# The second feed-forward as seven block products a tile, its residual kept in DRAM

## The chip, the cores and the metric

The kernel runs on one core of a Trainium2 chip and computes one decoder layer. The metric is the device time of one execution in microseconds (us); the time before is the median of three runs. Engines are named as the profile names them: PE is TensorE (matrix products, with its weight loads as PEld), DVE is VectorE, ACT is ScalarE, POOL is GpSimd, SP is SyncE, which starts most DMAs. SBUF and PSUM are the core's two on-chip memories; PE writes into PSUM, in 8 banks of 512 fp32 columns.

## The reference, cut to what matters

```python
def swiglu(u, w_in, w_out):
    ...                          # silu(u @ gate half of w_in) * (u @ up half of w_in), then @ w_out

def decoder_layer(x, c, lp, attend, s0_re, s0_im):
    ...
    h = x + 0.5 * g1[:, None, :] * swiglu(rms_modulate(x, lp['norm_ffn1'], sh1, sc1),
                                          lp['ffn1_w_in'], lp['ffn1_w_out'])
    ...                          # token mixer: attention and a state space model
    h = h + 0.5 * g3[:, None, :] * swiglu(rms_modulate(h, lp['norm_ffn2'], sh3, sc3),
                                          lp['ffn2_w_in'], lp['ffn2_w_out'])
```

The model width is 1024, the feed-forward's inner width 2816. There are 1024 prompt tokens and 64 tokens of samples, held together as T = 1092 columns (four are zeros). Everything is fp32 in DRAM.

## The kernel before, in words

Activations lie feature by partition: x is [128, 8, 1092], 8 tiles of 128 features (KD = 8). fp32 precision is had from fp16 products: each operand is scaled by a power of two and split into a high and a low fp16 part, and a product is three passes, high·high, high·low and low·high (`passes`, L155). `split` (L92) makes the parts: ACT writes the high one (L94), DVE the low one (L95).

The second feed-forward (`ffn`, L376, called at the end of the kernel) has 22 tiles of the inner width. `up(i)` (L382) makes one: a gate product and an up product, each over 8 k-tiles, 3 passes and 3 chunks of the columns (364, 364 and 360 wide) into one PSUM tile of three banks (`unit`, L165, matmul at L171, two such tiles). ACT takes the silu of the gate (L387), DVE multiplies it with the up product (L390) and takes the absolute maximum of the tile h (L395, `hm`). The first two tiles go chunk by chunk (`up_two`, L400), after the norm's chunks.

The inner width is worked off in three parts, PARTS (L26): tiles 0 to 10, 11 to 17, 18 to 21. When a part's tiles are there, `halves` (L424) takes the part's maximum over the partitions on POOL (L81), and splits each h into fp16 parts in a new slot of the pool hp3 (tag h, 17 slots, L1439). `down(0)` (L436) multiplies the first part with its rows of w_out, one tile of x after the other, and `add_gated` (L354) adds the result to x in SBUF. One more tile, tile 11, goes ahead of `down(0)` to cover the splitting, and `halves(1)`, `halves(2)`, `down(1)` and `last_part` (L461) stand at the end. The first feed-forward is the same code with 15 slots (L1320).

Weights come in groups of up to 1 MB (`Weights`, L99): fetched by SP two groups ahead into two slots wf, measured by DVE (L88), POOL (L81) and three short DVE instructions (L73 to L75), and split one group ahead into two slots each of wh and wl. So `next()` for tile i issues the split of tile i + 1.

Each engine runs its own queue in order. The order in the queues is settled when the program is built, by a scheduler that goes by modelled times and by which slots are free; the code only gives the dependencies. `after_mix` (L1417) makes the operand u of the second feed-forward from x, chunk by chunk, at the end of the mixer (`modulate_chunk`, L309).

Of the kernel before, what the change touches and what calls it, by code (L numbers as in the profile page):

```python
# [20 lines left out]
P = 128  # L21
# [4 lines left out]
PARTS = ((0, 11), (11, 18), (18, 22))  # L26
# [6 lines left out]
T = 3 * CH  # L33
EPS = 1e-6
# [34 lines left out]
def pow2_scale(k, m, pool=None, tag="sc", bufs=8):  # L69
# [21 lines left out]

def split(k, hi, lo, src, s):  # L92
    """hi + lo = s * src to 22 bits."""
    r = k.nc.scalar.activation(hi, src, AF.Copy, scale=s)  # L94
    k.nc.vector.scalar_tensor_tensor(lo, src, s, hi, op0=ALU.mult, op1=ALU.subtract)  # L95
    return r.ins


class Weights:  # L99
    """The groups of weights in the order in which they are used: split one ahead, loaded and measured two ahead.  # L100
    The last group of a product, of twice the size, is kept in slots of the scope's own, aside from the ring."""
# [5 lines left out]
    def fetch(self):  # L107
        k = self.k
        src, nk, nm, *aside = self.order.pop(0)
        wf = []  # L110
        for part in [src[:, :nk // 2], src[:, nk // 2:]] if aside else [src]:
# [3 lines left out]
        self.fetched.append((wf, nm, bool(aside)))  # L115

    def measure(self):
# [3 lines left out]
        for i, f in enumerate(wf):  # L121
# [38 lines left out]
def width(c, first):  # L160
    """Columns of chunk c that a pass takes: the zeros after the last token only need the first one."""
# [3 lines left out]
def unit(k, w, cols, act, nk):  # L165
    """One output tile: [P, 3, CH] of PSUM = sum over nk k-tiles of w[:, :, cols]^T act."""
# [9 lines left out]
def product(k, ps, w, cols, act, nk, c):  # L176
    """ps [P, CH] = chunk c of the columns of such a tile."""
# [37 lines left out]
def ada_part(k, dr, part, queue=None, then=None):  # L215
    """mods[:, part * 8 + tile, sequence]: one part of the modulation."""
# [25 lines left out]
def norm_coef(k, i, gain):  # L242
    """Modulation i as u * s = n * A + B, with s a power of two: A, B and 1 / s."""
# [9 lines left out]
    s, inv = pow2_scale(k, allmax(k, bound), k.co, f"ns{i}", 1)  # L253
# [9 lines left out]
def square_sums(k, x, c):  # L263
    """The sums of squares of the columns of chunk c of x [P, KD, T]: PSUM [4 x 32 equal rows, CH / 4]."""
# [12 lines left out]
def rstd_chunk(k, x, c, ss=None):  # L277
    """1 / rms of these columns, on all partitions: PSUM [P, CH]."""
# [6 lines left out]
    # the inverse square root: half the exponent's bits, then Newton's steps  # L285
# [16 lines left out]
def normalize_chunk(k, x, c, bc=None):  # L302
    """x[:, :, chunk c] to unit root mean square, in place."""
# [43 lines left out]

def scaled_gate(k, gate, iv):
# [5 lines left out]
def add_gated(k, xm, ps, g):  # L354
    """xm [P, T] += g * ps, g [P, NSQ] by sequence, ps [P, 3, CH]."""
# [12 lines left out]
def ffn_order(wi, wo):  # L368
    o = [(wi[i], KD, 256) for i in range(NFF)]
    a, b, c = wo  # L370
    oa = [(a[m], 11, P) for m in range(KD)]
    ob = [(b[g], 7, 256) for g in range(KD // 2)]
    return o[:12] + oa + o[12:] + ob + [(c, 4, D, True)]


def ffn(k, x, u, ivu, gate, fill, after_chunk, between=None):  # L376
    """x += gate * SwiGLU(u); after_chunk(c) is called when the columns of chunk c are complete."""
# [22 lines left out]
    def up_two():  # L400
        """The first two tiles, chunk by chunk of the columns."""
# [59 lines left out]
def last_part(k, x, gate, act, inv, behind, after_chunk):  # L461
    """x += gate * product of the last four k-tiles, chunk by chunk of the columns."""
# [46 lines left out]
def vec_exp(k, pool, x):  # L509
    """exp of a small tile [P, NG] by range reduction and a polynomial."""  # L510
# [16 lines left out]
def ssm_params(k, dr, sp, co):  # L527
    """The transition's powers and the discretized input matrix."""
# [1004 lines left out]
```

## Time and profile before

| | |
|---|---|
| median of 3 runs | 2501.14 us (2498.15 to 2502.89) |
| span of the profiled execution | 2513.7 us, 12.6 above that median |
| PE busy | 2430.5 us, 97% of the span |
| DVE, ACT, POOL busy | 56%, 31%, 7% |
| second feed-forward | the last 750 us or so of the span |

The page states no other time for the profiled execution than its span. How to read it: the span runs from the first instruction to the last on the slowest core; busy shares are of that span. The clock in a profile's window is the TensorE clock that was granted, as a share of full speed. "Idle before" in a row is the time the engine waited just before those instructions, with what ended the wait.

### The profile page before, as it was taken

Reading aid. Unit: us, or ns where it says so; the run is one execution under the profiler, and the core shown is the slowest. Engines: PE = TensorE matmul, PEld = TensorE weight load, DVE = VectorE, ACT = ScalarE, POOL = GpSimd, SP = SyncE. Lnnn points to the kernel's source line nnn. Section 1 sums busy time; section 2 is a strip of 40 time slices with the busy share of each in tenths; the row PEclk is TensorE's granted clock in tenths of the full one; section 3 lists DMA queues with packets and bytes.
Section 4 is the critical chain, followed back from the end, with each engine's and each line's share of the span. In section 5 each row is a group of like instructions: output and inputs, shape, how many; then the busy total and the mean of one; then the engine's idle time right before and its main releaser. Section 6 shows DMA issues by size and latency. Waiting matters only on the chain.

```text
span 2513.7 us, 38505 instructions
## 1 busy us (share of the span) xinstructions
PE 2430.5 (97%) x16615; PEld 1456.6 (58%) x16615; DVE 1417.2 (56%) x2637; ACT 782.4 (31%) x905; POOL 168.2 (7%) x249
## 2 busy tenths in 40 slices
PE   6999999999999999999999899999999999999997
PEld 2555566666656565775444444655666656666564
DVE  4522355458676744638889787697333353333545
ACT  3311122111122432146778676324211221111303
POOL 0111000000000000001133200000000000000000
PEclk8999999999999999889999999999999999999999
DMA  9644101112112234444133214520111111111112
GB/s 349 220 184 168 51 24 55 62 62 88 59 57 99 89 98 147 104 149 157 66 110 104 96 41 148 210 68 18 34 51 51 36 47 62 51 48 35 45 35 72
DMA packets 81946, 229.41 MB, mean 91 GB/s; under 512 B 11680, under 2 KB 45856, under 8 KB 72560
## 3 DMA queue, kind: packets, MB, share of 16 engines
q1 hardware_dynamic: 67952, 179.96, 21.0%
q0 software_dynamic: 13376, 46.70, 5.3%
q8 instruction: 130, 2.13, 0.3%
q10 hardware_dynamic: 448, 0.29, 0.1%
q14 instruction: 40, 0.33, 0.0%
HBM read 190.68 MB, written 36.24 MB: 90 GB/s over the span
## 4 chain that ended last, share of the span: by engine, by line
PE 42%; DVE 6%; ACT 4%; issue 2%; DMA 1%; another core or an unknown queue 1%; POOL 0%; DVEq 0%; POOLq 0%; ACTq 0%
PE u L171 27%; PE u L181 8%; PE z L850 2%; PE o L868 1%; PE P L787 1%; DVE mx L88 1%; PE P L863 1%; DVE h L95 1%; DVE wl L95 1%; DMA wf<-in_w_in 0%; ACT tmp L325 0%; DMA wf<-in_w_out_b 0%; ACT ae L857 0%; PE z L911 0%
## 5 line engine op out<-in xcount | busy, mean ns | idle before, releaser
L171 PEld LDWEIGHTS <-wh 128*128 128x128 f16 x6144 | 589.3, 97 | 387.3 <-issue 38.5
L171 PE MATMUL u<-u,wh 128*128 128x364 f16 (+1 forms) x4032 | 740.6, 317 | 0.0
L171 PE MATMUL u<-u,wl 128*128 128x364 f16 (+1 forms) x2016 | 420.1, 315 | 0.0
L181 PE MATMUL u<-u,wh 128*128 128x364 f16 (+1 forms) x1632 | 393.5, 319 | 12.0 <-ACT u L327 6.3
L171 PEld LDWEIGHTS <-wl 128*128 128x128 f16 x3072 | 298.9, 98 | 176.1 <-issue 2.6
L94 ACT ACTIVATE wh<-wf,sc 128x2048 f16<-128x2048 f32 (+3 forms) x92 | 172.1, 1871 | 681.8 <-PE u L171 616.5
L88 DVE TENSOR_REDUCE mx<-wf 128x1 f32<-128x2048 f32 (+3 forms) x98 | 208.7, 2131 | 250.3 <-DMA wf<-in_ffn_w_in 156.6
L171 PE MATMUL u<-h,wh 128*128 128x364 f16 (+1 forms) x1728 | 315.7, 317 | 9.9 <-DVE h L95 6.1
L181 PE MATMUL u<-u,wl 128*128 128x364 f16 (+1 forms) x816 | 260.2, 319 | 1.1 <-DVE wl L95 1.1
L181 PEld LDWEIGHTS <-wh 128*128 128x128 f16 x1824 | 176.5, 98 | 126.0 <-issue 28.6
L390 DVE SCALAR_TENSOR_TENSOR h<-u,iv,sil 128x1092 f32<-128x1092 f32 x40 | 54.2, 1354 | 331.6 <-PE u L171 293.8
L95 DVE SCALAR_TENSOR_TENSOR wl<-wf,sc,wh 128x2048 f16<-128x2048 f32 (+3 forms) x92 | 200.7, 2182 | 47.3 <-ACT wh L94 46.8
L81 POOL PARTITION_ALL_REDUCE am<-mx x106 | 49.4, 472 | 1966.7 <-DVE mx L88 1880.2
L171 PE MATMUL u<-h,wl 128*128 128x364 f16 (+1 forms) x864 | 180.1, 316 | 0.0
L387 ACT ACTIVATE sil<-u,iv 128x1092 f32<-128x1092 f32 x40 | 46.9, 1171 | 385.3 <-PE u L171 385.3
L181 PEld LDWEIGHTS <-wl 128*128 128x128 f16 x912 | 89.4, 98 | 69.8 <-issue 18.5
L181 PEld LDWEIGHTS <-aside 128*128 128x128 f16 x864 | 83.0, 97 | 50.4 <-issue 1.2
L181 PE MATMUL u<-h,aside 128*128 128x364 f16 (+1 forms) x576 | 90.9, 317 | 0.0
L358 DVE SCALAR_TENSOR_TENSOR x<-u,gt,x 128x728 f32<-128x728 f32 x40 | 38.8, 971 | 87.7 <-PE u L171 87.7
L227 PE MATMUL s<-aw,cs 128*32 128x256 f32 x576 | 64.8, 406 | 11.2 <-DMA aw<-in_ada_w 11.1
L857 ACT ACTIVATE ae<-z,bias,csqk 128x512 f32<-128x512 f32 (+3 forms) x96 | 62.9, 666 | 40.7 <-PE z L855 18.8
L858 DVE TENSOR_SCALAR az<-z,csqk,bias 128x512 f32<-128x512 f32 (+3 forms) x96 | 64.4, 674 | 8.8 <-ACT ae L857 8.2
(375 smaller groups left out, 2583.5 us busy)
## 6 DMA issues: line engine op xcount, KB each, us to landing
wf<-in_ffn_w_in SPq DMA_DIRECT2D x44, 1024.0 KB, 4.9
aw<-in_ada_w POOLq DMA_DIRECT2D x56, 512.0 KB, 6.6
wf<-in_w_in SPq DMA_DIRECT2D x16, 1024.0 KB, 5.6
wf<-in_ffn_w_out_a SPq DMA_DIRECT2D x16, 704.0 KB, 4.1
x<-in_xT SPq DMA_DIRECT2D x6, 1456.0 KB, 14.1
sg<-gd SPq DMA_DIRECT2D x16, 546.0 KB, 5.5
aw<-in_ada_w SPq DMA_DIRECT2D x16, 512.0 KB, 8.3
gd<-gate SPq DMA_DIRECT2D x45, 182.0 KB, 1.9
```

The source lines that it names most:

```text
L81: k.nc.gpsimd.partition_all_reduce(r, m, P, ABSMAX)
L88: k.nc.vector.tensor_reduce(m, src, axis=axis, op=ALU.max, apply_absolute_value=True)
L94: r = k.nc.scalar.activation(hi, src, AF.Copy, scale=s)
L95: k.nc.vector.scalar_tensor_tensor(lo, src, s, hi, op0=ALU.mult, op1=ALU.subtract)
L171: k.nc.tensor.matmul(ps[:, c, :n], wt[:, cols], act(kt, part)[:, c * CH:c * CH + n], start=kt == 0 and j == 0, stop=kt == nk - 1 and j == 2)
L181: k.nc.tensor.matmul(ps[:, :n], wt[:, cols], act(kt, part)[:, c * CH:c * CH + n], start=kt == 0 and j == 0, stop=kt == nk - 1 and j == 2)
L227: nc.tensor.matmul(ps[32 * i:32 * i + 32, :], k.cs[:, 4 * kk + j, :], ws[i][:, j, :], start=kk + j == 0, stop=kk == 1 and j == 3)
L387: nc.scalar.activation(c3(sil), pg, AF.Silu, scale=iv)
L390: nc.vector.scalar_tensor_tensor(c3(h), pu, iv, c3(sil), op0=ALU.mult, op1=ALU.mult)
L850: nc.tensor.matmul(ps[:, :n], a[r, P * j:P * j + P], b[r, cols], start=i == 0, stop=True, skip_group_check=True)
L857: nc.scalar.activation(ae[:, h, :n], ps[:, :n], AF.Abs, scale=inv, bias=b)
L858: nc.vector.tensor_scalar(az[:, h, :n], ps[:, :n], inv, b, op0=ALU.mult, op1=ALU.add)
```

## The change

It touches the second feed-forward, and PARTS for both.

- PARTS becomes 10, 8 and 4 tiles, so tile 10 is the one ahead of `down(0)`.
- Tiles 0 to 3 of the second feed-forward stay plain products, now in PSUM tiles of two banks (`pair_tile`, three of them), and for tiles 2 and 3 by halves of the columns (546, as matmuls of 272 and 274 columns to either side of the bank's border).
- Tiles 4 to 21 are seen as a 2 x 2 block product: rows gate and up, inner blocks of 4 k-tiles, columns in two halves. Seven block products of 4 k-tiles x 3 passes take the place of eight (`seven_products`), accumulated in three PSUM tiles X, Y and Z, with five additions on DVE, one copy and two silus on ACT and a last multiply on DVE.
- These need sums of weights, four DVE instructions of 512 columns a tile and 1536 more columns to split (`Weights.seven`; the layout reorders the weights into blocks), and sums of x, made once during tiles 2 and 3 (`Factors.sums`): 16 DVE sums of 546 columns and 8 splits of 1092, kept in 8 slots of the pool.
- `modulate_chunk` now works in place in x. So x goes to DRAM first (xd, three DMAs), `down(0)` reads each row tile from there and writes it back, and x is loaded again after the last of the seven products of tile 21. x's SBUF becomes a second pool of 8 slots, hq4 (`after_sums`).
- The maximum of |h| is replaced by a sum of |h| on ACT (`abs_bound`), and some scales are four times smaller (`lead=12`).

The diff, without the hunks that only remove comments and without repeated plumbing:

```diff
-PARTS = ((0, 11), (11, 18), (18, 22))
+PARTS = ((0, 10), (10, 18), (18, 22))
...
+def abs_bound(k, src, out):
+    junk = k.tmp().rearrange("p a n -> p (a n)").bitcast(BF16)[:, :src.shape[1]]
+    k.nc.scalar.activation(junk, src, AF.Abs, accum_out=out)
...
+        seven = aside == "seven"
+        fs = [wf[0][:, :1024], wf[0][:, 1024:]] if seven else wf
+        for i, f in enumerate(fs):
             absmax(k, f, mx[:, i:i + 1])
-        m = absmax(k, mx) if aside else mx[:, :1]
-        self.loaded.append((wf, nm, aside, *pow2_scale(k, allmax(k, m))))
+        m = absmax(k, mx) if len(fs) > 1 else mx[:, :1]
+        self.loaded.append((wf, nm, aside, *pow2_scale(k, allmax(k, m), lead=12 if seven else 14)))
...
+        if aside == "seven":
+            self.ready.append((self.seven(wf[0], s), inv, False))
+            return
...
+    def seven(self, f, s):
+        k = self.k
+        v = k.nc.vector
+        a11, a12, a22, a21 = (f[:, i:i + 512] for i in range(0, 2048, 512))
+        t, t4 = (k.tmp().rearrange("p a n -> p (a n)") for _ in range(2))
+        s3, s2, s4 = t[:, :512], t[:, 512:1024], t4[:, :512]
+        v.tensor_sub(s3, a11, a21)
+        v.tensor_add(a21, a21, a22)
+        v.tensor_sub(s2, a21, a11)
+        v.tensor_sub(s4, a12, s2)
+        h, l = (k.wp.tile([P, 2048], F16, tag=t_, bufs=2) for t_ in ("wh", "wl"))
+        split(k, h, l, f, s)
+        h3, l3 = (k.w3.tile([P, 1536], F16, tag=t_, bufs=2) for t_ in ("w3h", "w3l"))
+        split(k, h3[:, :1024], l3[:, :1024], t[:, :1024], s)
+        split(k, h3[:, 1024:], l3[:, 1024:], s4, s)
+        cut = lambda a, i: a[:, 512 * i:512 * i + 512]
+        r = {n: (cut(h, i), cut(l, i)) for i, n in enumerate(("a11", "a12", "a22", "s1"))}
+        r.update({n: (cut(h3, i), cut(l3, i)) for i, n in enumerate(("s3", "s2", "s4"))})
+        return r
...
+def pair_tile(k):
+    return k.psu.tile([P, 1024], F32, tag="u", bufs=3)
+def halves_unit(k, w, cols, act, nk):
+    for h in range(2):
+        ps = pair_tile(k)
+        a0 = h * HT - 240
+        for kt in range(nk):
+            for j, (wt, part) in enumerate(passes(w, kt)):
+                for a, b in ((240, 512), (512, 786)):
+                    k.nc.tensor.matmul(ps[:, a:b], wt[:, cols], act(kt, part)[:, a0 + a:a0 + b],
+                                       start=kt == 0 and j == 0, stop=kt == nk - 1 and j == 2)
+        yield h, slice(h * HT, h * HT + HT), ps[:, 240:786]
...
+        t = src if keep else k.tmp()[:, :nk, :n]
...
+    def sums(self, k, x, g):
+        nc = k.nc
+        v = nc.vector
+        a, b = (k.sum_slot() for _ in range(2))
+        q = x.rearrange("p (q k) (h n) -> p k q h n", q=2, h=2)[:, g]
+        v.tensor_sub(a[:, 0], q[:, 0, 1], q[:, 0, 0])
+        v.tensor_sub(a[:, 1], q[:, 1, 1], q[:, 0, 1])
+        v.tensor_sub(b[:, 0], q[:, 1, 1], a[:, 0])
+        v.tensor_sub(b[:, 1], q[:, 1, 0], b[:, 0])
+        for src in (a, b):
+            t = k.factor_slot()
+            nc.scalar.activation(t[:, :, 0], src, AF.Copy)
+            v.tensor_sub(t[:, :, 1], src, t[:, :, 0])
+            self.t.append(t)
...
+def seven_products(k, w, fac, iv, h):
+    nc = k.nc
+    v = nc.vector
+    view = lambda t: t[:, 240:786]
+    def add(t, a, b, first):
+        ah, al = w[a]
+        act = fac.get(b)
+        for kt in range(4):
+            for j, (wt, part) in enumerate(((ah, 0), (ah, 1), (al, 0))):
+                for c0, c1 in ((240, 512), (512, 786)):
+                    nc.tensor.matmul(t[:, c0:c1], wt[:, kt * P:kt * P + P], act(kt, part)[:, c0 - 240:c1 - 240],
+                                     start=first and kt == 0 and j == 0, stop=kt == 3 and j == 2,
+                                     skip_group_check=True)
+    q = k.sum_slot()
+    u2 = k.u2.tile([P, HT], F32, tag="u2", bufs=2)
+    p1, u3 = q[:, 0], q[:, 1]
+    h1, h2 = h[:, :HT], h[:, HT:]
+    X = pair_tile(k)
+    add(X, "a11", "b11", True)
+    nc.scalar.activation(p1, view(X), AF.Copy)
+    Y = pair_tile(k)
+    add(Y, "s2", "t2", True)
+    v.tensor_add(u2, view(Y), p1)
+    add(X, "a12", "b21", False)
+    nc.scalar.activation(h1, view(X), AF.Silu, scale=iv)
+    add(Y, "s3", "t3", False)
+    v.tensor_add(u3, view(Y), p1)
+    Z = pair_tile(k)
+    add(Z, "s1", "t1", True)
+    v.tensor_add(u3, view(Z), u3)
+    add(Y, "a22", "t4", False)
+    v.tensor_add(p1, view(Y), p1)
+    add(Z, "s4", "b22", False)
+    v.tensor_add(h2, view(Z), u2)
+    nc.scalar.activation(h2, h2, AF.Silu, scale=iv)
+    hh = h.rearrange("p (a n) -> p a n", a=2)
+    v.scalar_tensor_tensor(hh, q, iv, hh, op0=ALU.mult, op1=ALU.mult)
...
+def ffn_seven(k, fac, ivu, gate, xu, xd, after_sums, after_chunk):
+    nc = k.nc
+    hs, hm = {}, {}
+    act = lambda kt, part: fac.u[:, kt, part, :]
+    def bound(i):
+        p = [a <= i < b for a, b in PARTS].index(True)
+        if p not in hm:
+            hm[p] = k.small.tile([P, 12], F32, tag="hm", bufs=3)
+        j = i - PARTS[p][0]
+        abs_bound(k, hs[i], hm[p][:, j:j + 1])
+    def up(i):
+        w = k.w.next()
+        iv = mul_small(k, w[1], ivu)
+        h = hs[i] = k.h_slot(i, [P, T], F32, "h")
+        if i >= PLAIN:
+            seven_products(k, w[0], fac, iv, h)
+        else:
+            for _, cols, ps in halves_unit(k, w, slice(0, P), act, KD):
+                nc.scalar.activation(h[:, cols], ps, AF.Silu, scale=iv)
+            for _, cols, ps in halves_unit(k, w, slice(P, 2 * P), act, KD):
+                nc.vector.scalar_tensor_tensor(h[:, cols], ps, iv, h[:, cols], op0=ALU.mult, op1=ALU.mult)
+        bound(i)
...
+    def halves(p):
+        a, b = PARTS[p]
+        s, inv = pow2_scale(k, allmax(k, absmax(k, hm[p][:, :b - a])), tag="sh", bufs=3)
+        parts = []
+        for i in range(a, b):
+            h2 = k.h_slot(i, [P, 2, T], F16, "h2")
+            ins = split(k, h2[:, 0, :], h2[:, 1, :], hs[i], s)
+            if i - a < 6:
+                behind = ins
+            parts.append(h2)
+        return lambda kt, part: parts[kt][:, part, :], inv, behind
+    def down(p, hact, inv, behind, rows):
+        nk = PARTS[p][1] - PARTS[p][0]
+        per = 1 + p
+        last = [behind, behind]
+        for m in range(KD):
+            if m % per == 0:
...
+                iv = mul_small(k, w[1], inv)
+            xm, done = rows(m, last[m])
+            g = scaled_gate(k, gate[:, m, :], iv)
+            for h, _, ps in halves_unit(k, w, slice(m % per * P, m % per * P + P), hact, nk):
+                ins = add_gated_half(k, xm, h, ps, g)
+            last.append(ins)
+            done()
+    def row(m, after):
+        t = k.hp.tile([P, T], F32, tag="h", name="xr")
+        with k.tc.issue_after(after):
+            nc.sync.dma_start(t, xd[:, m, :])
+        return t, lambda: nc.sync.dma_start(xd[:, m, :], t)
+    up_two()
+    for i in range(2, PLAIN):
+        up(i)
+        n = 4 // (PLAIN - 2)
+        for g in range(n * (i - 2), n * (i - 1)):
+            fac.sums(k, xu, g)
+    after_sums()
+    for i in range(PLAIN, PARTS[0][1] + 1):
+        up(i)
+    down(0, *halves(0), row)
+    for i in range(PARTS[0][1] + 1, NFF):
+        up(i)
+    x = k.up.tile([P, KD, T], F32, tag="u", name="x")
+    for m in range(KD):
+        nc.sync.dma_start(x[:, m, :], xd[:, m, :])
+    h1, h2 = halves(1), halves(2)
+    down(1, *h1, lambda m, _: (x[:, m, :], lambda: None))
+    last_part(k, x, gate, *h2, lambda c: after_chunk(c, x))
...
-            modulate_chunk(k, x, box["cf"], box["u"], c, rstd_chunk(k, x, c))
-        with again(name="ring3", bufs=4) as k.ring:
+            nc.sync.dma_start(xd[:, :, c * CH:(c + 1) * CH], x[:, :, c * CH:(c + 1) * CH])
+            modulate_chunk(k, x, box["cf"], box["u"], c, rstd_chunk(k, x, c), keep=True)
...
+            k.h_slot = lambda i, shape, dt, name: (k.hp if i < 4 or 12 <= i < 17 else k.hq).tile(shape, dt, tag="h",
+                                                                                                 name=name)
+            xs2 = ExitStack()
+            def after_sums():
+                xs.close()
+                k.hq = xs2.enter_context(again(name="hq4", bufs=8, side="right"))
```

## Rows read from the trace of the kernel before

**Rows 1.** Page, part 1: busy us, share of the span, instructions, by engine.
```profile
PE 2430.5 (97%) x16615; PEld 1456.6 (58%) x16615; DVE 1417.2 (56%) x2637; ACT 782.4 (31%) x905; POOL 168.2 (7%) x249
```

**Rows 2.** Stretch table: length; PE, PEld, DVE, ACT, POOL busy (count); clock, DMA.
```profile
1800.00:2514.00 714.00, 693.46 (x4625) 433.76 (x4623) 295.52 (x427) 128.85 (x107) 13.47 (x34) 0.99 0.14 48
```

**Rows 3.** Timeline of PE within one tile: start, us, what, count.
```profile
2166.06 1.09 PE L171 MATMUL u<-u,wh 128*128 128x364 f16 x6
2166.99 0.62 PE L171 MATMUL u<-u,wl 128*128 128x364 f16 x3
...
2171.61 1.09 PE L171 MATMUL u<-u,wh 128*128 128x364 f16 x6
```

**Rows 4.** PE in the mixer, 256 columns: timeline, and its weight loads grouped.
```profile
1088.02 0.38 PE L1107 MATMUL z<-wh,u 128*128 128x256 f16 x2
...
1091.95 0.38 PE L1107 MATMUL z<-wh,u 128*128 128x256 f16 x2
L1107 PEld LDWEIGHTS <-u 128*128 128x128 f16 x384 | 37.9, 99 | 5.5 <-issue 0.4
```

**Rows 5.** DVE groups by form: count, busy us, mean ns of one, idle before.
```profile
L88 DVE TENSOR_REDUCE mx<-wf 128x1 f32<-128x2048 f32 x72 | 164.3, 2283 | 186.0 <-DMA wf<-in_ffn_w_in 156.6 <-DMA wf<-in_ffn_w_out_c 18.2 <-DMA wf<-in_w_in 9.5
L95 DVE SCALAR_TENSOR_TENSOR wl<-wf,sc,wh 128x2048 f16<-128x2048 f32 x66 | 154.8, 2345 | 41.0 <-ACT wh L94 40.4
L390 DVE SCALAR_TENSOR_TENSOR h<-u,iv,sil 128x1092 f32<-128x1092 f32 x40 | 54.2, 1354 | 331.6 <-PE u L171 293.8 <-PE s L618 26.3 <-issue 11.5
L358 DVE SCALAR_TENSOR_TENSOR x<-u,gt,x 128x728 f32<-128x728 f32 x40 | 38.8, 971 | 87.7 <-PE u L171 87.7
L784 DVE SCALAR_TENSOR_TENSOR ae<-ae,csqk,ah 128x1024 f16<-128x1024 f32 x24 | 33.7, 1405 | 2.7 <-issue 1.6 <-DVE az L778 0.5
L778 DVE TENSOR_TENSOR az<-az,ae 128x512 f32<-128x512 f32 x12 | 8.2, 682 | 0.0
L417 DVE SCALAR_TENSOR_TENSOR h<-u,iv,sil 128x364 f32<-128x364 f32 x12 | 7.0, 592 | 16.7 <-ACT sil L416 16.7
```

**Rows 6.** ACT groups by form, the same columns.
```profile
L94 ACT ACTIVATE wh<-wf,sc 128x2048 f16<-128x2048 f32 x66 | 132.1, 2001 | 453.8 <-PE u L171 390.7 <-PE u L181 35.0 <-DVE sc L75 22.2
L94 ACT ACTIVATE h<-h,sh 128x1092 f16<-128x1092 f32 x44 | 50.6, 1197 | 49.5 <-DVE h L95 34.4 <-DVE sh L75 14.7
L780 ACT ACTIVATE ah<-ae,csqk 128x1024 f16<-128x1024 f32 x24 | 27.5, 1144 | 2.4 <-DVE ae L777 1.9
L416 ACT ACTIVATE sil<-u,iv 128x364 f32<-128x364 f32 x12 | 6.5, 553 | 16.0 <-PE u L181 16.0
```

**Rows 7.** Timeline of DVE in tile 20: one measurement of weights and its wait.
```profile
2329.80 2.02 DVE L88 TENSOR_REDUCE mx<-wf 128x1 f32<-128x1792 f32 x1 [4.43 <-DMA wf<-in_ffn_w_out_b]
```

**Rows 8.** Timeline of ACT and of DVE about the start of `down(0)`.
```profile
2006.40 5.57 ACT L94 ACTIVATE h<-h,sh 128x1092 f16<-128x1092 f32 x5
2019.16 1.21 ACT L94 ACTIVATE h<-h,sh 128x1092 f16<-128x1092 f32 x1 [7.18 <-DVE h L95]
2016.51 1.35 DVE L390 SCALAR_TENSOR_TENSOR h<-u,iv,sil 128x1092 f32<-128x1092 f32 x1 [11.56 <-PE u L171]
2017.78 1.34 DVE L95 SCALAR_TENSOR_TENSOR h<-h,sh 128x1092 f16<-128x1092 f32 x1
```

**Rows 9.** Timeline of PE at the starts of `down(0)` and `down(1)`.
```profile
2019.18 1.06 PE L171 MATMUL u<-h,wh 128*128 128x364 f16 x3 [2.31 <-DVE h L95]
...
2366.27 0.62 PE L171 MATMUL u<-h,wh 128*128 128x364 f16 x3 [1.05 <-DVE h L390]
2367.53 0.62 PE L171 MATMUL u<-h,wh 128*128 128x364 f16 x3 [0.64 <-DVE h L95]
```

**Rows 10.** Busy time by stretch after that first wait, columns as in rows 2.
```profile
2019.00:2022.00 3.00, 2.82 (x10) 1.44 (x10) 3.00 (x4) 1.58 (x2) 0.00 (x0) 0.50 0.00 0
```

**Rows 11.** Page, part 6: DMA issues, KB each, us to landing.
```profile
wf<-in_ffn_w_in SPq DMA_DIRECT2D x44, 1024.0 KB, 4.9
sg<-gd SPq DMA_DIRECT2D x16, 546.0 KB, 5.5
```

More of the change, by code (lines that the diff above doesn't have):

```diff
@@ L33 @@
 T = 3 * CH
+HT = T // 2
 EPS = 1e-6
@@ L49 @@
 class K:
+    pass
 class Pool:
@@ L348, in scaled_gate, with add_gated_half @@
+def add_gated_half(k, xm, h, ps, g):
+    v = k.nc.vector
+    n = NP - HT if h else HT
+    a = xm[:, h * HT:h * HT + n]
+    v.scalar_tensor_tensor(a, ps[:, :n], g[:, 0:1], a, op0=ALU.mult, op1=ALU.add)
+    if h:
+        st = k.small.tile([P, NB, LS], F32, tag="st", bufs=2)
+        v.tensor_mul(st, by_seq(ps[:, n:n + NS]), seq_bc(g[:, 1:]))
+        s = by_seq(xm[:, NP:NP + NS])
+        return v.tensor_add(s, s, st).ins
 def scaled_gate(k, gate, iv):
@@ L450, in ffn @@
     up_two()
-    for i in range(2, 12):
+    for i in range(2, PARTS[0][1] + 1):
         up(i)
     down(0, *halves(0))
-    for i in range(12, NFF):
+    for i in range(PARTS[0][1] + 1, NFF):
         up(i)
@@ L469, in last_part @@
         n = min(CH, NP - c * CH)
-        for m0 in range(0, KD, 3):
-            ms = range(m0, min(m0 + 3, KD))
-            ps = k.psu.tile([P, 3, 512], F32, tag="u", bufs=k.nunits)
+        per = 2 if k.pairs else 3
+        for m0 in range(0, KD, per):
+            ms = range(m0, min(m0 + per, KD))
+            ps = (pair_tile(k).rearrange("p (q n) -> p q n", q=2) if k.pairs else
+                  k.psu.tile([P, 3, 512], F32, tag="u", bufs=k.nunits))
             for q, m in enumerate(ms):
@@ L485, in last_part, with up_two @@
         after_chunk(c)
+def ffn_seven(k, fac, ivu, gate, xu, xd, after_sums, after_chunk):
[20 more added lines that the diff above has]
+        bound(i)
+    def up_two():
+        ws = [k.w.next() for _ in range(2)]
+        ivs = [mul_small(k, w[1], ivu) for w in ws]
+        for i in range(2):
+            hs[i] = k.h_slot(i, [P, T], F32, "h")
+        for c in range(3):
+            for i in range(2):
+                ps = pair_tile(k).rearrange("p (q n) -> p q n", q=2)
+                for q in range(2):
+                    product(k, ps[:, q, :CH], ws[i], slice(q * P, q * P + P), act, KD, c)
+                h = c3(hs[i])[:, c]
+                nc.scalar.activation(h, ps[:, 0, :CH], AF.Silu, scale=ivs[i])
+                nc.vector.scalar_tensor_tensor(h, ps[:, 1, :CH], ivs[i], h, op0=ALU.mult, op1=ALU.mult)
+        for i in range(2):
+            bound(i)
+    def halves(p):
[15 more added lines that the diff above has]
+            if m % per == 0:
+                if m == 0:
+                    with k.tc.issue_after(behind):
+                        w = k.w.next()
+                else:
+                    w = k.w.next()
+                iv = mul_small(k, w[1], inv)
[20 more added lines that the diff above has]
+    down(0, *halves(0), row)
+    for i in range(PARTS[0][1] + 1, NFF):
+        up(i)
[5 more added lines that the diff above has]
+    last_part(k, x, gate, *h2, lambda c: after_chunk(c, x))
@@ L1274, in trunk_kernel @@
     k.nc, k.tc = nc, tc
-    k.nunits = 2
+    k.nunits, k.pairs = 2, False
     pool = lambda **kw: ctx.enter_context(open_pool(tc, **kw))
@@ L1372, in prep0 @@
         def prep0():
+            zt = sp.tile([P, (TC - 1) * GC], F32, tag="zt", bufs=1)
             nc.vector.memset(zt, 0.0)
```

76 lines of the change are left out of this document (47 added, 29 removed).

## The prediction

> **What bounds the kernel now.** I first read the busy shares: PE is busy for 97% of the span and DVE for 56% [rows 1]. Shares over a whole span hide stages, so I then read the stretch that the change works on. From 1800 us to the end PE is busy 693.46 of 714 us, DVE 295.52 and ACT 128.85, and the granted clock is 0.99 [rows 2]. Here every microsecond of matrix work is a microsecond of time, and the other two engines have room. Third, what PE's work is made of: within a tile, nine matmuls (six with the high weights, three with the low) are one k-tile of 1092 columns, and four such groups take 2171.61 - 2166.06 = 5.55 us [rows 3], so a k-tile costs 1.3875 us and one pass of it 462.5 ns. A tile is 16 of these: 22.2 us, with no gap. There are few waits to win back here. The largest stand at the start of down(0), 2.31 us, and of down(1), 1.05 and 0.64 us, where splits of h were not ready [rows 9]. So the change must be judged by PE's work that it takes away, and by the waits that it puts in PE's way.
>
> **The change part by part.**
>
> *Seven products for eight.* I need the pitch of matmuls of 272 and 274 columns, which the kernel doesn't have. Its neighbours are 364/360 at 1387.5 / 9 = 154.2 ns (362.7 columns on average) [rows 3] and 256 columns, of which 36 start between 1088.02 and 1091.95, so 109.2 ns [rows 4]. The line between the two is 0.422 ns a column, and at 273 columns gives 116.4 ns. A pair is 232.8 ns, a seven-product tile has 7 x 4 x 3 = 84 pairs, 19.55 us. Against 22.2 that is 2.65 us less, and over 18 tiles 47.7 us. Each matmul loads its own weights (as many loads as matmuls [rows 1]); a load takes 99 ns and at 256 columns stays hidden [rows 4], so it does at 273.
>
> *Four matmuls for three elsewhere.* A pass over 1092 columns is now two pairs, 465.6 ns, 3.1 more than 462.5. In down(0) and down(1) there are 18 x 3 x 8 = 432 of these, +1.3 us, in tiles 2 and 3 96, +0.3. PE's sum is -46.1 us.
>
> *DVE and ACT in a tile.* All the extra work lies beside PE, as long as it fits in 19.55 us. DVE: four sums of 512 at 0.68 = 2.7; low parts of 2048, 1024 and 512 columns at 2.35, 1.41 and about 0.8 (from the 1024 and 364 rows) = 4.6; the measurement 2.3 in two pieces, so about 2.4; five evictions of 546 columns at 0.78 (half way between 0.592 at 364 and 0.971 at 728) = 3.9; the multiply 1.35. That is 14.9 us and some short ones [rows 5]. ACT: high parts 2.0 + 1.14 + 0.65, a copy and two silus of 546 columns at about 0.73 (between 0.553 at 364 and 1.197 at 1092), the sum of |h| 1.2: 7.2 us [rows 6]. Both fit on paper. But DVE also stands still in front of each measurement, 4.43 us in the tile shown, until its weights land [rows 7] (4.9 us a group [rows 11]). Nobody minds that today. In the new tile it would bring DVE to 19.4 us, just PE's time, if nothing fills the wait.
>
> *The new waits inside a tile.* Before, PE filled one PSUM tile for 11.1 us while the other was read. Now products accumulate onto a PSUM tile just read: X gets its second product one product (24 matmuls, 2.79 us) after its first ended, and ACT's copy of 0.73 us must lie in between; Y and Z give DVE the same 2.79 us three times, for 0.78 us of work. The slack is some 2.0 us. Behind what can these stand in their queues? On DVE behind a low part, 2.35 us: 0.35 late, or behind a measurement that waits for its DMA, up to 4.43 us: 2.4 late. On ACT behind the high parts of the next group. If these wait for nothing they take 3.8 us from the start of the tile and the copy starts at 3.8, ends at 4.5, before 5.6. If they in turn wait for the sums on DVE, and these for the last multiply of the tile before (0.78 + 0.73 + 1.35 us after that tile's last product, 2.9), the sums end at 5.6 and the high parts of 2048 and 1024 columns at 8.7 at the latest, so the copy is up to some 3.8 us late. The bounds are 0 and 3.8 us a tile. I take 0.5: the queues' order goes by modelled times, most of the extra work is ready long ahead, and the nearest certain lateness is the 0.35 us. 18 x 0.5 = +9.
>
> *Start of down(0).* Before, five high parts of h were ready early, as many as there were free slots, at 2006.40, but the first low part came only behind the multiply of the covering tile, at 2017.78, and the sixth high part at 2019.16, when a slot was freed [rows 8]. PE lost 2.31 us there and worked at half clock (1.2 GHz) from 2019 to 2022 [rows 9, 10]; that is some 4 us in all. This gets worse: h of tiles 4 to 10 and their splits share eight slots, seven of them taken by h, so from the sixth k-tile on high and low part go one after the other, 1.2 + 1.35, about 2.6 us each; and the first half of the columns needs a k-tile every 0.7 us instead of 1.39. With the low parts behind the multiply, 3 us after the tile, the first five are there at 3 + 5 x 1.35 = 9.8 us, the tenth at 22.8; PE would have needed it at 6.3. So up to 16 us against the 4 of before, +12, and some clock behind it. If the splits run during tile 10 (19.55 us, of which DVE needs 13.5 for ten low parts and some 8 for its own), little is lost: 0 at best, or -4 if the old wait goes too. I take +11, as the rows of before show the late order.
>
> *Start of down(1).* Eight k-tiles at 1.35 us against a need every 0.7: 8 x 1.35 + 4.4 = 15.2 against 5.6, so some 9.5 us where 1.7 stand now. Bounds -2 and +8; I take +5.5, since half of those eight k-tiles find free slots early.
>
> *First seven-product tile.* Four sets of sums of x: per set four sums of 546 (about 0.72) and two low parts of 1092 (1.3), 5.5 us of DVE, 22 in all, and 9 us of ACT, during tiles 2 and 3 (44.6 us), where DVE has some 14 us of its own and 10 for tile 4's weights. It just fits. Bounds 0 and 15; I take +3.
>
> *The residual's DMAs.* x goes out in three transfers on SP's queue, after each chunk is complete; the in-place modulation of that chunk must wait for it. The nearest transfer takes 5.5 us [rows 11]; only the last chunk is on the path, so 0 to +5.5. I take +0.5, as the transfer starts together with the norm's own chain (sums of squares, inverse root, broadcast), for which the modulation waits anyway. Rows for down(0) come one tile of 14 us ahead, 5.5 us each; the 4.4 MB of reload lie under tile 21's end and the slow start of down(1): nothing. Uncovered, each would cost its 5.5 us once. The first feed-forward has the same products with 10 and 8 k-tiles instead of 11 and 7: 0 (plus or minus 1). The changed scales add no instruction.
>
> *Sum.* -46.1 + 9 + 11 + 5.5 + 3 + 0.5 = -17.1 us. Against the span, 2513.7 to 2496.6. The median lies 12.6 us below the span; I carry the difference over unchanged: 2501.1 - 17.1 = 2484.
>
> **A rule that speaks against it.** The rows say 109.2 ns at 256 columns and 154.2 at 362.7 [rows 3, 4], close to the slope of 2.4 GHz. The Trainium skill, "TensorE: Matmul & The Clock Gate", section "Back-to-back issue gap", gives for a sustained stream of loads and matmuls about 81 ns at 128 columns and 131 at 512, so that columns cost little and a matmul much. By an estimate on that line a pair would be 200 ns and a tile 16.8 us, against 16.1 for the plain one: a loss of 0.7 us a tile. The trace doesn't agree with it at either width.
>
> **The rivals.**
>
> *The copy behind the splits (slower).* ACT's copy of X stands each time behind the high parts of the next group, and these behind DVE's sums and the multiply of the tile before. For it: before, too, high parts sit at the start of a tile in ACT's queue, and low parts of h waited 10 us behind a multiply that they don't need [rows 8]. Against it: the sums only need weights that are there early. Price: about 3 us a tile instead of 0.5, 18 x 2.5 = +45, to 2529. It decides from 46.1 - 20 = 26 us, or 1.45 us a tile.
>
> *DVE is the bound (no change).* DVE's 14.9 us with 4.43 of waits and late evictions give a tile of 20.5 us: 1 us lost a tile, +18 instead of +9, and with both downs at their upper ends (+20 for +16.5) the sum is -5: 2496, at most 2503. For it: the four deadlines of 2.0 us. Against it: the idle time of DVE before was only idle for want of other work.
>
> *It doesn't do what it says (slower).* A tile has 168 matmuls now where it had 144. If a narrower matmul weren't cheaper, 168 at 154.2 ns would be 25.9 us, 3.7 more than 22.2: +67 over 18 tiles, and with the +19.5 of the waits 2588. The gain is gone from 22.2 / 168 = 132 ns on. The 256-column rows, 109.2 ns, speak against it. The rule above is a milder form of the same.
>
> **How the numbers follow.** Forecast 60% (2459 to 2495), DVE as bound 13%, the copy behind the splits 25%, paid by number 2%. The forecast's low end has no wait in the tiles and 2 us more at each down: -46.1 + 2 + 2 = -42, 2459. The range goes to the slower case's price: 2459 to 2530. Within 0.2% (2496.1 to 2506.1), about what a measurement of this kernel can tell from no change, lies most of the second case. Faster 0.62, same 0.11, slower 0.27. The likeliest case alone has 2459 to 2495.
>
> **What would show it.** Matmuls of 272 and 274 columns some 116 ns apart, and 19.55 us of PE busy in a tile. Tile pitch (start of one multiply to the next) 20.0 us: right; 19.6: no waits; over 21: a rival. PE's wait in a tile before the second product into X, released by ACT, is the copy; before the products into Y and Z, released by DVE, the evictions. PE idle at the two downs released by the low parts, 16 and 9 us, with half clock behind. Wrong would be idle time somewhere that I gave nothing: the row transfers, the end of the mixer, or the first feed-forward.

## The result

The changed kernel takes 2532.88 us (median of 4 runs, 2528.32 to 2539.52) against 2499.64 (2497.37 to 2502.89): 1.013 times the time before, 95% interval 1.0112 to 1.0149. It is slower by 33 us, where 17 us less were forecast, and 3 us beyond the range.

The profile after, first the shares (as in [rows 1]: busy us, share of the span, instructions):

```profile
PE 2397.7 (95%) x17575; PEld 1551.5 (61%) x17575; DVE 1556.7 (62%) x2877; ACT 861.9 (34%) x1031; POOL 169.5 (7%) x249
```

PE is busy for 33 us less than before (46 us less work were forecast; matmuls at a lower clock count as busy for longer), but the span is longer. The next view is one of the matmuls of the seven products and their weight loads (line 444), grouped: how long the engine sat idle ahead of them, how often, and who ended it. The row "issue" belongs to the weight loads (PEld); the others are PE's.

```profile
its engine sat idle before it (us, times) until:
  issue: 48.2, 32
  ACT q L454: 30.0, 16
  ACT fac L419: 5.1, 3
  DVE q L461: 4.3, 5
  DVE mx L89: 2.3, 6
```

L454 is ACT's copy of the first product. Now one tile, on PE (start, us, what, count, idle before and who ended it), on ACT and on DVE. X's products read u with wh and wl; Y's first reads fac, the sums of x, with w3h and w3l, the sums of weights; Z's first reads fac with wh and wl.

```profile
2301.64 0.39 PE L444 MATMUL u<-u,wl 128*128 128x272 f16 x2
2301.87 0.63 PE L444 MATMUL u<-fac,w3h 128*128 128x272 f16 x4
...
2304.45 0.39 PE L444 MATMUL u<-fac,w3l 128*128 128x272 f16 x2
2304.68 0.63 PE L444 MATMUL u<-fac,wh 128*128 128x272 f16 x4
2305.15 0.39 PE L444 MATMUL u<-fac,wl 128*128 128x272 f16 x2
2305.38 0.63 PE L444 MATMUL u<-fac,wh 128*128 128x272 f16 x4
...
2307.25 0.39 PE L444 MATMUL u<-fac,wl 128*128 128x272 f16 x2
2309.78 0.63 PE L444 MATMUL u<-u,wh 128*128 128x272 f16 x4 [2.13 <-ACT q L454]
```

```profile
2302.01 0.75 ACT L469 ACTIVATE h<-h,iv 128x546 f32<-128x546 f32 x1 [11.09 <-DVE h L468]
2304.19 1.11 ACT L96 ACTIVATE tmp<-h 128x1092 bf16<-128x1092 f32 x1 [1.42 <-DVE h L471]
2305.21 0.19 ACT L96 ACTIVATION_READ_ACCUMULATOR tmp<-h 128x1 f32 x1
2305.57 2.00 ACT L101 ACTIVATE wh<-wf,sc 128x2048 f16<-128x2048 f32 x1 [0.17 <-issue]
2307.47 1.74 ACT L101 ACTIVATE w3h<-tmp,sc 128x1024 f16<-128x1024 f32 x2
2309.12 0.60 ACT L454 ACTIVATE q<-u 128x546 f32<-128x546 f32 x1
```

```profile
2302.80 1.35 DVE L471 SCALAR_TENSOR_TENSOR h<-q,iv,h 128x1092 f32<-128x1092 f32 x1 [0.82 <-ACT h L469]
2304.07 0.68 DVE L162 TENSOR_TENSOR tmp<-wf 128x512 f32<-128x512 f32 x1
2304.79 0.69 DVE L163 TENSOR_TENSOR wf<-wf 128x512 f32<-128x512 f32 x1
```

The last multiply of the tile before (L471) ends at 2304.15. Only then come the sum of |h| on ACT (L96) and the sums of weights on DVE (L162 on). The high parts of the next group follow, 2305.57 to 2309.2, and the copy comes last, at 2309.12. X's first product had ended by 2301.9. Behind it PE worked off Y's first and, which the code has later, Z's first as well; it was through with both at 2307.6 and stands until 2309.78. Six matmuls of 272 and 274 columns start every 0.70 us (2304.68 to 2305.38): 116.7 ns each.

The granted clock of four tiles, from one last multiply to the next (columns as in [rows 2]):

```profile
2256.58:2280.22 23.64, 21.51 (x170) 17.12 (x168) 14.61 (x20) 6.84 (x8) 0.36 (x1) 0.93 0.13 46
2280.22:2302.80 22.58, 20.02 (x170) 16.33 (x168) 14.51 (x22) 6.84 (x8) 0.36 (x1) 1.00 0.15 47
2302.80:2325.14 22.34, 20.00 (x170) 16.32 (x168) 14.23 (x17) 6.83 (x8) 0.35 (x1) 1.00 0.14 48
2325.14:2350.04 24.90, 22.76 (x181) 18.16 (x179) 16.60 (x19) 8.84 (x9) 0.36 (x1) 0.93 0.15 46
```

From one multiply to the next these take 22.3 to 24.9 us (the last stretch holds 181 matmuls, a tile 168), where 20.0 were forecast and a plain tile of before took 22.2. The shorter ones have the waits alone, the longer ones a stretch of lower clock as well. And the start of down(0), answering to [rows 8, 9]:

```profile
2001.41 1.21 ACT L101 ACTIVATE h<-h,sh 128x1092 f16<-128x1092 f32 x1 [0.51 <-DVE h L102]
2002.68 1.11 ACT L96 ACTIVATE tmp<-h 128x1092 bf16<-128x1092 f32 x1
2003.70 0.19 ACT L96 ACTIVATION_READ_ACCUMULATOR tmp<-h 128x1 f32 x1
2003.79 4.48 ACT L101 ACTIVATE h<-h,sh 128x1092 f16<-128x1092 f32 x4
```

```profile
1997.77 0.40 PE L444 MATMUL u<-u,w3l 128*128 128x272 f16 x2
2005.03 1.52 PE L231 MATMUL u<-h,wh 128*128 128x272 f16 x6 [6.86 <-ACT h L101]
```

Six of the ten splits ran one after the other, the last from 2001.41. The other four, those of tiles 0 to 3, which are the first k-tiles that PE needs, come last, behind the sum of |h| of tile 10.

### The profile page after: what moved, and what is told of

The parts are those of the page before. It is cut to its first block, busy times and chain, and to the rows that moved or that the text cites. A ratio compares the mean times of both kernels' runs of the same rounds, so it can differ in the third digit from the quotient of the medians.

```text
span 2526.1 us, 40840 instructions
## 1 busy us (share of the span) xinstructions
PE 2397.7 (95%) x17575; PEld 1551.5 (61%) x17575; DVE 1556.7 (62%) x2877; ACT 861.9 (34%) x1031; POOL 169.5 (7%) x249
## 4 chain that ended last, share of the span: by engine, by line
PE 32%; DVE 12%; ACT 5%; DMA 4%; issue 2%; POOL 0%; DVEq 0%; POOLq 0%; ACTq 0%
PE u L215 9%; PE u L231 7%; PE u L444 6%; DMA wf<-in_ffn_w_in 3%; PE u L205 3%; DVE mx L89 2%; PE z L1097 2%; DVE wl L102 2%; ACT wh L101 1%; PE o L1115 1%; PE P L1034 1%; DVE h L471 1%; PE P L1110 1%; PE z L1158 1%; DVE h L468 1%
## 5 line engine op out<-in xcount | busy, mean ns | idle before, releaser
L215 PE MATMUL u<-u,wh 128*128 128x364 f16 (+1 forms) x1632 | 392.9, 319 | 11.1 <-ACT u L378 6.3
L205 PE MATMUL u<-u,wh 128*128 128x364 f16 (+1 forms) x2112 | 392.6, 317 | 0.0
L101 ACT ACTIVATE wh<-wf,sc 128x2048 f16<-128x2048 f32 (+2 forms) x92 | 172.1, 1871 | 506.6 <-PE u L205 317.1
L89 DVE TENSOR_REDUCE mx<-wf 128x1 f32<-128x2048 f32 (+2 forms) x116 | 209.8, 1822 | 209.8 <-DMA wf<-in_ffn_w_in 122.5
L215 PE MATMUL u<-u,wl 128*128 128x364 f16 (+1 forms) x816 | 259.8, 319 | 1.1 <-DVE wl L102 1.1
L102 DVE SCALAR_TENSOR_TENSOR wl<-wf,sc,wh 128x2048 f16<-128x2048 f32 (+2 forms) x92 | 200.9, 2184 | 62.3 <-ACT wh L101 61.5
L205 PEld LDWEIGHTS <-wl 128*128 128x128 f16 x1680 | 163.5, 98 | 97.1 <-issue 3.6
L205 PE MATMUL u<-u,wl 128*128 128x364 f16 (+1 forms) x1056 | 220.7, 316 | 0.0
L231 PE MATMUL u<-h,wh 128*128 128x274 f16 (+1 forms) x1152 | 183.6, 281 | 8.7 <-ACT h L101 8.0
L205 PE MATMUL u<-h,wh 128*128 128x364 f16 (+1 forms) x864 | 157.3, 317 | 5.2 <-DVE h L102 3.4
L215 PEld LDWEIGHTS <-wl 128*128 128x128 f16 x912 | 89.1, 98 | 69.1 <-issue 18.3
L444 PE MATMUL u<-u,wh 128*128 128x272 f16 x576 | 98.3, 294 | 30.1 <-ACT q L454 30.0
L231 PE MATMUL u<-h,wl 128*128 128x272 f16 (+1 forms) x576 | 114.3, 279 | 0.0
```

Source lines behind the costliest of these rows:

```text
L89: k.nc.vector.tensor_reduce(m, src, axis=axis, op=ALU.max, apply_absolute_value=True)
L205: k.nc.tensor.matmul(ps[:, c, :n], wt[:, cols], act(kt, part)[:, c * CH:c * CH + n], start=kt == 0 and j == 0, stop=kt == nk - 1 and j == 2)
L215: k.nc.tensor.matmul(ps[:, :n], wt[:, cols], act(kt, part)[:, c * CH:c * CH + n], start=kt == 0 and j == 0, stop=kt == nk - 1 and j == 2)
L231: k.nc.tensor.matmul(ps[:, a:b], wt[:, cols], act(kt, part)[:, a0 + a:a0 + b], start=kt == 0 and j == 0, stop=kt == nk - 1 and j == 2)
L444: nc.tensor.matmul(t[:, c0:c1], wt[:, kt * P:kt * P + P], act(kt, part)[:, c0 - 240:c1 - 240], start=first and kt == 0 and j == 0, stop=kt ...
```

## The experiments

**Theory A**: ACT's copy stands behind the high parts of the next group, these behind DVE's sums, these behind the last multiply of the tile before, because the slots of hp4 (the pool of 17 slots, hp3 before) are given out in the order of the code. **Theory B**: DVE is the bound, and a wait taken away in one place comes back at another eviction (an engine's reading of a PSUM tile). Each kernel is compared with the kernel before on the same chip. Chips differ: before takes 2511.17 us on that of e1 to e4 and 2511.41 on that of e5 to e7, some 11 us more than in the result above, so times in us are to be read against these.

**e1_late.** The split of the next group is asked for behind the copy:

```diff
     nc.scalar.activation(p1, view(X), AF.Copy)
+    k.w.one()                    # split and load the next group
...
-        w = k.w.next()
+        w = k.w.ready.pop(0) if i >= PLAIN else k.w.next()
```

> The changed kernel, with one thing moved: the split of the next group of weights is asked for after ACT's copy of the first product instead of at the tile's start, so it takes its slots and its places in the queues behind that copy. Theory A (the copy stands in ACT's queue behind the next group's high parts, which stand behind DVE's sums, which stand behind the last multiply of the tile before): the wait of 2.3 us before the second product into X goes, the tile pitch falls from 22.3 to 23.6 us to about 20, and some 17 x 2.6 = 44 us are won, so about 2490. Theory B (DVE is the bound, 16 us of work and waits for weights between four deadlines): the wait only moves to the evictions, the pitch stays at 22 or more, 2525 to 2535.

Measured: 0.994 of before (0.992 to 0.996), 2496.4 us. ACT's queue in a tile:

```profile
2239.68 1.11 ACT L96 ACTIVATE tmp<-h 128x1092 bf16<-128x1092 f32 x1 [1.42 <-DVE h L479]
2240.71 0.19 ACT L96 ACTIVATION_READ_ACCUMULATOR tmp<-h 128x1 f32 x1
2240.80 0.60 ACT L461 ACTIVATE q<-u 128x546 f32<-128x546 f32 x1
2241.30 1.99 ACT L101 ACTIVATE wh<-wf,sc 128x2048 f16<-128x2048 f32 x1
```

The copy (now L461) is ahead of the high parts, and the pitch, from one tile's start to the next, is 20.1 us. Theory A. The start of down(0) is as before the move, 6.47 us of waiting.

**e2_junk.** The unused output of the sum of |h| gets a slot of its own:

```diff
-    junk = k.tmp().rearrange("p a n -> p (a n)").bitcast(BF16)[:, :src.shape[1]]
+    junk = k.u2.tile([P, T], BF16, tag="jk", bufs=1, name="junk")
...
-    u2 = k.u2.tile([P, HT], F32, tag="u2", bufs=2)
+    u2 = k.u2.tile([P, HT], F32, tag="u2", bufs=1)
```

> The changed kernel; the unused output of the sum of |h| gets a slot of its own instead of one of hp4's (u2 has one buffer instead of two to make room). Theory A with the slots as its cause (hp4's slots are given out in the code's order, so the sums of the next group's weights get theirs only after the sum of |h| of the tile before, hence after its last multiply): the sums run before that multiply, the high parts are out of the copy's way, the pitch falls to 20 to 20.5, 2490 to 2500. If the sums stand behind the multiply for another reason, nothing changes: 2533, plus or minus 3. Theory B: 2525 to 2535.

Measured: 0.9926 (0.9904 to 0.9947), 2489.93 us. The same queue, and below it on DVE the end of a tile's last multiply (L471) and the first sum of weights behind it:

```profile
2225.77 0.75 ACT L469 ACTIVATE h<-h,iv 128x546 f32<-128x546 f32 x1 [0.48 <-DVE h L468]
2226.56 0.63 ACT L454 ACTIVATE q<-u 128x546 f32<-128x546 f32 x1
2228.23 1.11 ACT L96 ACTIVATE junk<-h 128x1092 bf16<-128x1092 f32 x1 [1.04 <-DVE h L471]
...
2241.36 2.00 ACT L101 ACTIVATE wh<-wf,sc 128x2048 f16<-128x2048 f32 x1 [8.47 <-PE u L444]
```

```profile
2226.84 1.35 DVE L471 SCALAR_TENSOR_TENSOR h<-q,iv,h 128x1092 f32<-128x1092 f32 x1
...
2228.77 0.69 DVE L162 TENSOR_TENSOR tmp<-wf 128x512 f32<-128x512 f32 x1
```

No instruction was moved in the code; a slot was added, and u2, a pool of its own, has one buffer less. The sums still follow a multiply, but one a whole tile earlier: the high parts made from them come 13 us later, when they wait for PE alone (for wh to come free), and are gone before the next copy. That is theory A with its cause in the slots. The pitch is 20.6, and the wait at down(0) falls to 1.73 us, since the first four splits no longer stand behind the sum of |h|.

**e3_plain.** All 22 tiles plain, the rest of the change in place:

```diff
-    o = [(wi[i], KD, 256, *(("seven",) if seven and i >= PLAIN else ())) for i in range(NFF)]
+    o = [(wi[i], KD, 256, *(("seven",) if seven and i >= NFF else ())) for i in range(NFF)]
...
-        if i >= PLAIN:
+        if i >= NFF:
             seven_products(k, w[0], fac, iv, h)
...
-        for g in range(n * (i - 2), n * (i - 1)):
-            fac.sums(k, xu, g)
```

> The changed kernel with all 22 tiles of the second feed-forward as plain products by halves of the columns: the seven products, the sums of weights and of x are left out, while the parts of 10, 8 and 4 tiles, the residual in DRAM, the eight slots, the smaller PSUM tiles and the sum of |h| on ACT stay. Both theories put the loss into the seven-product tiles: four matmuls for three cost 1.6 + 18 x 0.15 = 4 us, the start of down(0) some 4 us more than before, so about 2508. If the residual in DRAM and the slots carry the loss, it stays near 2533.

Measured: 1.0081 (1.0052 to 1.0111), 2530.8 us; some 20 us above before on its chip, where 8 were expected. From tile 2 on it takes 8.5 us more than before (table below), near the expected 8; the rest lies ahead of tile 2. So with the plain tiles the changed kernel loses some 20 us, and with seven products 32 (e6).

**e4_parts.** Only the parts of 10, 8 and 4 tiles:

```diff
-PARTS = ((0, 11), (11, 18), (18, 22))
+PARTS = ((0, 10), (10, 18), (18, 22))
...
-    for i in range(2, 12):
+    for i in range(2, 11):
...
-    for i in range(12, NFF):
+    for i in range(11, NFF):
```

> The kernel before with only the parts of 10, 8 and 4 tiles instead of 11, 7 and 4, in both feed-forwards. The same number of products of the same shapes: 2500, plus or minus 3, for both theories. If some 14 us of the loss come from outside the second feed-forward, as the difference of the two spans (12 us) against that of the medians (33 us) could mean, 2505 to 2515.

Measured: 1.0014 (1.0001 to 1.0027), 2514.04 us, 2.9 above before on its chip: within the plus or minus 3, at its edge.

**e5_before_again, e6_after_again.** Both kernels unchanged, on one chip, for profiles that can be compared.

> The kernel before, unchanged, for a profile from the same chip as the others of this set. In the profiles the second feed-forward of the changed kernel is 19 us longer than that of before (from tile 2 to the end 738.9 against 719.6), while the medians differ by 33. If the other 14 us lie in the code ahead of tile 2, this profile reaches tile 2 earlier than 1794 us, near 1780, and the changed kernel doesn't. If the first profile of before was taken in a slower execution, its span here is that much nearer to its times.

> The changed kernel, unchanged, on the same chip as the others: 1.013 times before. Both theories expect tile 2 to the end at 739 us again; what is left of the difference of the medians lies ahead of tile 2.

Measured: 1.0008 (0.9997 to 1.0018), 2512.02 us, and 1.0133 (1.0117 to 1.0148), 2542.98 us. On this chip the span of before is 2512.3 and its times agree with it. So the first profile of before, 2513.7, looks like one from such a chip, and the 12.6 us by which it exceeded its median say nothing of the kernel; on which chip it was taken isn't on record. Tile 2 starts at 1793.1 and 1797.4: 4 us of the loss lie ahead of it, 22 behind it. The spans differ by 26, the medians by 31; the 5 us between come from the executions that were profiled: that of e5 took 2514.28 us, 2.3 above its median, that of e6 2540.37, 2.6 below.

**e7_both.** The edits of e1 and e2 together.

> The changed kernel with both moves: the next group's split behind the copy of X, and a slot of its own for the unused output of the sum of |h|. Theory A: pitch 20.1 as with the late split, the start of down(0) with 2 us of waits as with the own slot instead of 7, so 8 to 12 us less than the better of the two: 0.989 of before. Theory B (DVE is the bound and each move only shifts the wait): no better than the own slot alone, 0.993.

Measured: 0.9888 (0.9869 to 0.9907), 2480.44 us: theory A. From tile 2 on (table below) e1 gains 41.5 us over e6, e2 52.1 and both together 60.2. So the two gains overlap for the most part: each takes the copy's wait out of the tiles. What e2 has beyond e1 lies at the start of down(0) and in the first two seven-product tiles; what e1 adds to e2 is 8 us in the tiles. What is left in a tile, on DVE:

```profile
2252.94 2.35 DVE L89 TENSOR_REDUCE mx<-wf 128x1 f32<-128x1024 f32 x2 [2.35 <-DMA wf<-in_ffn_w_in]
2255.20 0.72 DVE L472 TENSOR_TENSOR q<-u,q 128x546 f32<-128x546 f32 x1
```

The addition that PE waits for (L472) stands behind a measurement that itself waited 2.35 us for its weights.

**e8_measure.** As e7, the measurement queued behind the addition:

```diff
-            self.load()
+            if self.order:
+                self.fetch()
...
-    v.tensor_add(u3, view(Z), u3)
+    u3z = v.tensor_add(u3, view(Z), u3)
+    with k.tc.issue_after(u3z.ins):
+        if k.w.fetched:
+            k.w.measure()
```

> As e7, and the measurement of the next group's weights is queued on DVE behind the addition of Z to u3, no longer ahead of the additions that PE waits for. In e7 PE still waits some 10 us in all in the seven-product tiles, most of it 0.3 to 0.7 us a tile released by DVE, where a measurement (2.35 us and up to 2.1 of waiting for its weights) stands ahead of an addition. If that is their cause, 5 to 8 us less than e7: pitch 19.8, 0.986 of before. If the additions are late for another reason, as e7: 0.989.

Measured: 0.9864 (0.9843 to 0.9884), 2467.36 us on a chip where before takes 2501.54. It is the fastest of all, 34 us below before. From tile 2 on it takes 4.4 us less than e7 (9.7 less in the 18 tiles, 5.3 more in the downs, where its trace has 3.9 us of waits for splits); the intervals of the two ratios overlap. Its tiles 11 to 21 (columns as in [rows 2]):

```profile
2086.60:2303.20 216.60, 216.57 (x1850) 179.41 (x1848) 154.05 (x220) 72.00 (x85) 4.24 (x12) 1.00 0.17 57
```

PE has no gap left: 216.6 / 11 = 19.69 us a tile. The same eleven tiles in e6, and in e3, where they are plain:

```profile
2131.00:2378.60 247.60, 224.25 (x1849) 181.76 (x1848) 156.44 (x223) 73.53 (x84) 4.61 (x13) 0.98 0.15 50
```

```profile
2123.80:2370.80 247.00, 247.00 (x2114) 204.66 (x2112) 79.50 (x103) 52.17 (x56) 4.25 (x12) 1.00 0.15 50
```

247.6 and 247.0: in the changed kernel, the seven products gained nothing over plain tiles of the same layout. All that PE saves it loses again by waiting and by a lower clock.

The stages of all kernels, from the starts of PE's matmuls in their traces (us; e8 is from the faster chip, so its start of tile 2 can't be set against the others):

| kernel | tile 2 starts | from there to the span's end | a tile (last ten or eleven) | PE's longest wait at down(0) | time against before |
|---|---|---|---|---|---|
| before (e5) | 1793.1 | 719.2 | 22.2 | 2.32 | 1.0008 |
| changed (e6) | 1797.4 | 740.8 | 22.51 | 6.87 | 1.0133 |
| e1_late | 1797.9 | 699.3 | 20.11 | 6.47 | 0.994 |
| e2_junk | 1795.1 | 688.7 | 20.61 | 1.73 | 0.9926 |
| e3_plain | 1801.1 | 727.7 | 22.45 | 5.97 | 1.0081 |
| e4_parts | 1792.5 | 717.5 | 22.2 | 2.31 | 1.0014 |
| e7_both | 1795.8 | 680.6 | 20.14 | 1.74 | 0.9888 |
| e8_measure | 1787.7 | 676.2 | 19.69 | 0.41 | 0.9864 |

## Why the prediction was wrong

*What bounds the kernel.* Right, and the test holds at the end: where PE waits for nothing in the tiles (e8), tile 2 to the end is 43 us shorter than before, close to the 46 that PE's sum gave.

*Seven products for eight.* Right. 116.7 ns against 116.4, and 19.69 us a tile against 19.55. The rival by which matmuls are paid by number fell with it.

*Four matmuls for three.* Somewhat small: a plain tile takes 22.45 (e3) instead of 22.2, where 22.35 were forecast.

*DVE and ACT in a tile.* Right in size: in e8 DVE is busy 154.05 / 11 = 14.0 us a tile (forecast 14.9) and ACT 6.5 (7.2). DVE is not the bound, so that rival fell as well.

*The new waits inside a tile.* This is the step that failed: "I take 0.5". The changed kernel's tile takes 22.51 (e6) where 19.69 are possible (e8): 2.8 us lost a tile in the last eleven, which is 51 us for 18, where 9 were forecast. The rival that put the copy behind the splits had the mechanism step by step and its price, "about 3 us a tile". The text dismissed it because the sums "only need weights that are there early". That is true of the weights and not of the slot. A sum also needs room for its output, and hp4 gave that room only after the output of the sum of |h| had its own, which e2 shows by giving that output another place. The front told that the order goes by which slots are free; the prediction looked at slots for the splits of h alone, and not for the four temporary tiles of a seven-product tile. The working also sized the slack too strictly, by the code's order, with one product of 2.79 us between X's two. In PE's queue two stood there, and it didn't help: in the tile shown above the high parts were through only at 2309.2, some 8 us after the last product of the tile before (the prediction's bound had 8.7 at the latest).

*The clock.* The sum had no term for it in the tiles. Counted by the starts of the matmuls from tile 2 on, 124 matmuls ran at half clock (1.2 GHz) in e6 and 10 in e5; at some 0.11 us each that is 14 us against 1.5. In e6 ten tiles have the wait of 2.13 us; in five of them 14 or 15 matmuls at half clock follow, in the other five none.

*Start of down(0).* Forecast +11, for splits that run one after the other. PE waits 6.87 us in e6 against 2.32, and some 2 us at low clock follow, so about +5. The cause was another: the six splits in the small pool did run one after the other, but most of them during tile 10, near the more hopeful end of the bounds. The four in hp4 were late, again for a slot, and with e2's edit the wait is 1.73.

*Start of down(1).* Too dear: 5.5 forecast, no more than before measured (in e6 1.11 and 0.59 us, [rows 9] had 1.05 and 0.64).

*First seven-product tile.* The term itself came near: 5.1 us for the sums of x (L419), 4.2 in e6, 3 forecast. The tile took 33.1 us in e6 instead of 19.69, though, as the copy's largest wait, 4.2 us, and a stretch at half clock come on top. In e2 and e7 PE doesn't wait for the sums of x at all, in e1 4.9 us: this wait too went with the slot.

*The residual's DMAs.* No wait for a row or for the reload in any trace. But on the chips where before takes 2511 us, tile 2 starts 2 to 8 us later with the change than in e5, and the traces show a place for it, one that the sum gave nothing: the end of the mixer. PE's wait ahead of the branch products, before (e5) and after (e6):

```profile
1554.43 1.09 PE L171 MATMUL u<-ob,wh 128*128 128x364 f16 x6 [2.39 <-ACT gate L1120]
```

```profile
1567.85 1.97 PE L205 MATMUL u<-ob,wh 128*128 128x364 f16 x6 [6.16 <-DVE mt L1496]
```

In e6 DVE and ACT wait there too, until the gates sg have come from DRAM (ACT waits 6.71 us for them), and PE works at half clock from 1568 to 1572. All seven traces with the change have this wait, 5.7 to 6.2 us, and between 1530 and 1575 us they fall back by 5.0 to 5.9 us against e5; e4, with the parts alone, falls back by 0.8. Why the gates come later was not tested. What x's three transfers cost can't be told apart from the rest of the mixer and stays open.

*In sum*, from tile 2 on e6 loses 21.6 us: some 42 less work for PE (18 x (22.2 - 19.69) = 45 in the tiles, some 3 back in plain tiles and downs), so some 64 of waits and low clock more than before. The copy has 33 of them, counted from start to start of PE's matmuls in e6 (30.5 by the profile's idle times), the clock 12, the evictions 10; the rest are the sums of x and the start of down(0). That the rival's 2529 came within 4 us of the measured time is in part luck: it had neither the clock nor the end of the mixer, and it paid 11.5 us too much for the two downs.

## What to carry to other kernels

Where a tile of a pool is asked for decides when the work that writes it can start, even if its inputs are long there: list, for every temporary, what is asked for ahead of it in the same pool and when that is written. When a chain of products accumulates onto a tile that another engine has to read in between, put the reader ahead of all work for the next group in that engine's queue, and price the slack between both against the longest run of instructions that can stand there. Count that slack in the order of the queue, which can differ from that of the code. An optional output that nobody reads deserves a slot of its own.

## What the runs showed of the hardware

The same wait did not cost the same each time. Two tiles of the changed kernel with 2.13 us of waiting for the copy, one after the other: the stretches behind the first (columns as in [rows 2]), then both waits:

```profile
2264.00:2265.00 1.00, 1.00 (x11) 0.80 (x10) 1.00 (x2) 0.00 (x0) 0.00 (x0) 0.97 0.54 98
2265.00:2266.00 1.00, 1.00 (x7) 0.68 (x5) 1.00 (x2) 0.00 (x0) 0.00 (x0) 0.50 0.71 205
2266.00:2267.00 1.00, 1.00 (x6) 0.66 (x5) 0.23 (x1) 0.00 (x0) 0.00 (x0) 0.50 1.00 426
2267.00:2268.00 1.00, 1.00 (x7) 0.65 (x5) 0.00 (x0) 0.04 (x1) 0.00 (x0) 0.50 0.78 328
```

```profile
2263.57 0.63 PE L444 MATMUL u<-u,wh 128*128 128x272 f16 x4 [2.13 <-ACT q L454]
...
2287.20 0.63 PE L444 MATMUL u<-u,wh 128*128 128x272 f16 x4 [2.13 <-ACT q L454]
```

After the first the clock is full for more than a microsecond and then 0.50 for some three. After the second the whole tile has 1.00 (its row stands above: 2280.22 to 2302.80). So the loss from a wait of this length can't be read from the wait alone.
